# Three pairs of down tiles as seven products of quarters behind a plain part, in the two feed-forward blocks of a decoder step

## The chip, the cores and the metric

One NeuronCore of a Trainium2 chip runs the whole program. The metric is the device time of one execution in microseconds, the median of the runs shown. The profile is of one execution, taken by the hardware profiler; its times are counted from the start of its span. "Line" is a line of the kernel before, as the profile names it, if nothing else is said.

## What is computed

The program is one step of a hybrid decoder layer, in fp32, for 560 tokens at once: 512 of a prompt, 32 of running sequences and 16 meta tokens. Two feed-forward blocks (FFN1, FFN2) stand around a mixer of two attention branches. What matters here is this of the reference:

```
def swiglu(x, w_gate, w_up, w_down):
    return (jax.nn.silu(x @ w_gate) * (x @ w_up)) @ w_down

    h = x + 0.5 * rms_norm(swiglu(rms_norm(x, ffn1_pre_g), ffn1_w_gate, ffn1_w_up, ffn1_w_down), ffn1_post_g)
    ...
    y = h + 0.5 * rms_norm(swiglu(rms_norm(h, ffn2_pre_g), ffn2_w_gate, ffn2_w_up, ffn2_w_down), ffn2_post_g)
```

The model width is 1024 and the hidden width 2816. `@ w_down` is the down stage: 22 k-tiles of 128 hidden rows, and 8 tiles of 128 output columns.

## The kernel before

**Layout and precision.** Activations lie transposed, features on the 128 partitions and tokens along a row. A row of 560 tokens (544 in FFN2, which no longer needs the meta tokens) is cut in two halves, `h` = 0 and 1. Each fp32 factor is cut into a high part, rounded to fp32r by a cast on ScalarE, and the low rest, a subtraction on VectorE. A product of a weight tile and a moving tile is three matmuls: high by high, high by low, low by high.

**The down stage.** `k_steps` (lines 686 to 698) does one tile of output columns over a chunk of k-tiles. One k-tile is a **step**: six matmuls for both halves (lines 694 and 695 per half, then 697 per half), or three for one. `by_chunks` cuts each tile into chunks of 8, 7 and 7 k-tiles. The first two tiles go chunk by chunk side by side, since the hidden k-tiles 8 to 21 get their high and low parts only while those two run. Tiles 0 to 3 (0 to 4 in FFN2) are done for both halves; of the rest the first half is done for all tiles, then the second half for all, in the reverse order, so that the norm of the first half can start early. Its outputs come from `Norm`: `tile` squares and scales each finished tile on ScalarE (lines 738 and 739) and adds the squares up on VectorE; `start` sums them by matmuls with ones (lines 755 and 756) and takes the root; `add` scales and adds to `hT`, the residual h.

**What sets the order.** PE (TensorE), DVE (VectorE), ACT (ScalarE) and POOL run in the order in which the program is written; SP's transfers are ordered by a scheduler. `step()` is called after each k-tile and starts what `later(n, f)` had put off by n steps. The engines take their instructions in that order and wait by semaphores.

**Weights.** `Chunks` holds the list of weight tiles to come. `fetch` issues one transfer into one of three `raw` buffers (line 185, or two by line 620 for "quarters"). `split` casts the oldest raw to one of three `hi` buffers (ACT, line 660) and takes the `lo` part three steps later (DVE, line 152, the helper `tt`, which all two-operand operations share). In the down stage each chunk begins with one split and one fetch.

**Seven products.** The gate and up tiles and some gates of the mixer already use a product of two 2 x 2 block matrices in seven products instead of eight. The blocks of the moving matrix are a11, a21, a12, a22 (two halves of tokens by two halves of k), those of the weights two tiles by two halves of k. `weights_at` puts the four weight sums (DVE), the casts (ACT, line 855) and the lows at fixed steps; four sums s1 to s4 of moving blocks are made ahead; seven products of 4 k-tiles at 3 matmuls follow, in 14 steps, and their results are added up on DVE.

**h.** During the gate and up stage `hT`, 8 tiles of 128 x 560, is parked in DRAM (`h_dram`) and its room reused. `other_tiles` fetches it back in its last lines (line 1187), at the start of the down stage.

**Room.** `Arena` hands out pieces of SBUF ("room") by rules on which piece has been free longest. PSUM has two sets of four banks, "acc" and "ps".

Of the kernel before, what the change touches and what calls it, by code (L numbers as in the profile page):

```python
# [40 lines left out]
KEEP = 5  # L41
SUMS_BACK = (80, 86, 92, 102)
MIXER = [("R", "r", n) for n in range(3, 8)]
# [77 lines left out]
def hybrid_step(  # L121
# [158 lines left out]
    class Gates:  # L280


        def __init__(self, hd):
            self.hd = hd
# [415 lines left out]
    todo, vheld = [], []  # L700
    GATES, ROWS, EARLY = 6, 1, {3: 2}

    F0, F1 = (5, 13, 20), (5, 11, 14)
    LATE, MIX = (12, 22), (2, 4)

# [10 lines left out]
    def later(n, f):  # L716
        todo.append([n, f])
# [5 lines left out]
    class Norm:  # L723
# [37 lines left out]
        def add(self, h, g):  # L761
            w, n = self.wid[h], len(self.SETS[g])
            y, x = self.view(h, g), hT_room[g][:, : n * NT].rearrange("p (k t) -> p k t", t=NT)[:, :, h * HW : h * HW + w]
# [58 lines left out]
    def hidden(f, sl, at, nw, wid, hid, pairs):  # L822

        hi, lo = take(NT, F32R, True), take(NT, F32R, True)
        if pairs is None:
            for h, p in enumerate(zip(arena.halves(hi), arena.halves(lo))):
                hid.t[f, h] = p
        else:
            pairs[f] = hi, lo
            for h in range(2):  # L830
                c = slice(h * HW, h * HW + wid[h])
# [140 lines left out]
    def other_tiles(old, gain, rs, nw, wid, hid, pairs, plan, late, sums_at, begun):  # L972
# [210 lines left out]
        for i in range(len(waiting) + 3):  # L1183
            later(2 * i + 1, lambda: waiting and hidden(*waiting.pop(0), 1, nw, wid, hid, pairs))
        hT[:], hT_room = whole(KD)
        for k in range(KD):
            nc.sync.dma_start(hT[k], h_dram[k])

    CUTS = [(0, 8), (8, 15), (15, 22)]
    wd = ffn1_w_down[0]  # L1190

    order = [(n, (0, 1)) for n in range(4)] + [(n, (0,)) for n in range(4, 8)] + [(n, (1,)) for n in range(7, 3, -1)]
    DOWN = [(n, (0, 1)) for n in range(5)] + [(n, (0,)) for n in range(5, 8)] + [(n, (1,)) for n in range(7, 4, -1)]

    def by_chunks(order):

        both = [(n, hs, j) for j in range(3) for n, hs in order[:2]]
        return both + [(n, hs, j) for n, hs in order[2:] for j in range(3)]
# [4 lines left out]
    st.todo += [(wd, CUTS[j][0] * P, (CUTS[j][1] - CUTS[j][0]), P * n, P, False) for n, hs, j in by_chunks(order) if (n, hs) != (7, (1,))]  # L1203
    st.todo += [(win, r0, 4, c, 2 * P, 1 < n < 6) for n, (r0, c) in enumerate(vrows)]
# [12 lines left out]
    gate_up_weights(PLAN2, ffn2_w_gate[0], ffn2_w_up[0], 0)  # L1217
    st.todo += [(ffn2_w_down[0], CUTS[j][0] * P, (CUTS[j][1] - CUTS[j][0]), P * n, P, False) for n, hs, j in by_chunks(DOWN) if (n, hs) != (7, (1,))]
    E = mybir.EngineType
    with tc.manual_schedule(engines={E.PE, E.DVE, E.Activation, E.Pool}):  # L1220
# [164 lines left out]
        last, accs = {}, {}  # L1385
        for n, hs, j in by_chunks(order):
            if j == 0:
# [767 lines left out]
    with tc.manual_schedule(engines={E.PE, E.DVE, E.Activation, E.Pool}):  # L2155
# [222 lines left out]

        nd, last, accs = Norm(half2, W2), {}, {}
        ys = y_sample.rearrange("b t d -> (b t) d")  # L2380
# [11 lines left out]

        for n, hs, j in by_chunks(DOWN):
            if j == 0:
                accs[n, hs] = {h: ps("acc") for h in hs}
# [7 lines left out]
            k_steps(acc, parts, k0, k1, KF, hid, hs, wid=W2)  # L2403
            if j < 2:
                continue
            for h in hs:
                later(1, lambda n=n, h=h, acc=acc: nd.tile(n, h, acc[h]))
            if (n, hs) == (7, (0,)):
                later(2, exp_ln_table)
                later(F1[0], lambda: nd.start(0))  # L2410
                for g in range(3):
                    later(F1[1] + 12 * g, lambda g=g: nd.add(0, g))
                    for j in range(2):
                        later(F1[1] + 12 * g + 7 + 4 * j, lambda j=j, g=g: out(j, g))
        for p in pairs.values():
# [37 lines left out]
```

## Time and profile before

| | |
|---|---|
| median of 3 runs | 1515.96 us (1514.38 to 1517.47) |
| the profiled execution, its own time | 1509.63 us |
| its span, and mean granted TensorE clock | 1507.9 us, 0.999 |
| FFN1, down stage | 267.1 to 402.6 us of the span |
| FFN2, down stage | 1359.7 us to the tail, which begins at 1494.7 us |

The profile's page gives each engine's busy time and the chain of work that ended last, followed back from the end. Views of the trace give the rest: who waited for whom; stretches, with each engine's busy time, the granted clock and the DMA's share; groups of equal instructions, with their count, busy time and the mean duration of one in ns; and the instructions in order of time. There the first number of a row is its start, the second its duration (of all xN together), and what stands in brackets is the idle time of its engine just before, and what ended it. PE is TensorE, DVE VectorE, ACT ScalarE, SP the engine that issues most transfers.

### The profile page before, as it was taken

The numbers are of one execution on the slowest core, as the hardware profiler recorded it, in microseconds if no ns is written. First come the engines' busy times: TensorE is split into PE (matmuls) and PEld (weight loads), VectorE is DVE, ScalarE is ACT, GpSimd is POOL, SyncE is SP. The second block draws the span as 40 slices with busy tenths as digits, with TensorE's granted clock in tenths as the row PEclk, the third lists the DMA queues.
The fourth block names the chain that finished last, engine by engine and source line by source line (L and its number), as shares of the span: only waits on it lengthen the run. The fifth ranks groups of instructions, "written<-read, shape, count | busy, mean of one in ns | idle before, by whom it ended". The sixth has DMA issues, their size and how long they took to land.

```text
span 1507.9 us, 29580 instructions
## 1 busy us (share of the span) xinstructions
PE 1495.4 (99%) x11959; PEld 1444.0 (96%) x11959; DVE 1038.6 (69%) x1831; ACT 758.5 (50%) x1400; POOL 149.1 (10%) x216
## 2 busy tenths in 40 slices
PE   9999999999999999999999999999999999999998
PEld 8999999999999889899988999999999999999997
DVE  5888888523787857777776534977567888885234
ACT  6445454433665657565555443534564554544234
POOL 2000000000000111123224651000000000000000
PEclk9999999999999999999999999999999999999999
DMA  8123334524655473334455668434531343334343
GB/s 250 55 86 99 98 98 137 145 77 131 161 138 154 124 108 84 92 83 119 126 105 131 189 195 194 110 96 136 168 111 50 101 145 110 99 97 118 90 116 99
DMA packets 279561, 181.84 MB, mean 121 GB/s; under 512 B 10154, under 2 KB 264416, under 8 KB 279424
## 3 DMA queue, kind: packets, MB, share of 16 engines
q1 hardware_dynamic: 273968, 163.09, 41.0%
q0 software_dynamic: 5440, 16.85, 3.1%
q8 instruction: 94, 1.54, 0.4%
q14 instruction: 43, 0.35, 0.1%
q10 hardware_dynamic: 16, 0.00, 0.0%
HBM read 157.17 MB, written 22.74 MB: 119 GB/s over the span
## 4 chain that ended last, share of the span: by engine, by line
PE 95%; DVE 2%; DMA 1%; ACT 1%; issue 0%; SPq 0%; DVEq 0%; ACTq 0%
PE acc L694 10%; PE acc L697 10%; PE acc L695 10%; PE acc L681 8%; PE acc L1146 8%; PE acc L1144 8%; PE acc L1145 8%; PE acc L682 7%; PE acc L684 7%; PE acc L1087 2%; PE acc L1084 2%; PE acc L1085 2%; PE ps L1779 1%; PE acc L924 1%; PE acc L925 1%; PE acc L926 1%
## 5 line engine op out<-in xcount | busy, mean ns | idle before, releaser
L152 DVE TENSOR_TENSOR lo<-raw,hi 128x1024 fp32r<-128x1024 f32 (+1 forms) x216 | 258.6, 1198 | 174.8 <-ACT hi L660 166.3
L152 DVE TENSOR_TENSOR room<-room,room 128x544 fp32r<-128x544 f32 (+16 forms) x367 | 237.4, 669 | 122.4 <-ACT room L738 55.7
L681 PE MATMUL acc<-room,hi 128*128 128x280 f32 (+1 forms) x928 | 271.4, 309 | 0.1
L1146 PE MATMUL acc<-room,lo 128*128 128x280 f32 (+1 forms) x896 | 259.5, 290 | 0.0
L1145 PE MATMUL acc<-room,hi 128*128 128x280 f32 (+1 forms) x896 | 259.3, 289 | 0.0
L1144 PE MATMUL acc<-room,hi 128*128 128x280 f32 (+1 forms) x896 | 259.1, 289 | 0.0
L682 PE MATMUL acc<-room,hi 128*128 128x280 f32 (+1 forms) x928 | 250.5, 289 | 0.0
L694 PE MATMUL acc<-room,hi 128*128 128x280 f32 (+1 forms) x784 | 222.0, 292 | 0.0
L695 PE MATMUL acc<-room,hi 128*128 128x280 f32 (+1 forms) x784 | 219.0, 290 | 0.0
L660 ACT CAST hi<-raw 128x1024 fp32r<-128x1024 f32 (+1 forms) x130 | 131.9, 1015 | 145.0 <-PE acc L695 125.3
L684 PE MATMUL acc<-room,lo 128*128 128x280 f32 (+1 forms) x928 | 192.8, 289 | 0.0
L697 PE MATMUL acc<-room,lo 128*128 128x280 f32 (+1 forms) x784 | 192.3, 290 | 0.0
L681 PEld LDWEIGHTS acc<-room,hi 128*128 128x128 f32 x928 | 174.9, 188 | 13.0 <-issue 11.0
L682 PEld LDWEIGHTS acc<-room,hi 128*128 128x128 f32 x928 | 175.1, 189 | 2.8 <-issue 1.9
L1146 PEld LDWEIGHTS acc<-room,lo 128*128 128x128 f32 x896 | 168.6, 188 | 0.0
L1144 PEld LDWEIGHTS acc<-room,hi 128*128 128x128 f32 x896 | 168.6, 188 | 0.0
L1145 PEld LDWEIGHTS acc<-room,hi 128*128 128x128 f32 x896 | 168.4, 188 | 0.0
L694 PEld LDWEIGHTS acc<-room,hi 128*128 128x128 f32 x784 | 147.6, 188 | 2.0 <-issue 0.9
L695 PEld LDWEIGHTS acc<-room,hi 128*128 128x128 f32 x784 | 147.6, 188 | 0.2
L684 PEld LDWEIGHTS acc<-room,lo 128*128 128x128 f32 x928 | 145.0, 188 | 0.0
L855 ACT CAST hi<-raw 128x1024 fp32r<-128x1024 f32 x86 | 90.1, 1052 | 107.8 <-PE acc L1145 47.0
L697 PEld LDWEIGHTS acc<-room,lo 128*128 128x128 f32 x784 | 134.0, 188 | 0.0
(352 smaller groups left out, 2858.2 us busy)
## 6 DMA issues: line engine op xcount, KB each, us to landing
raw<-in_w_in_dram SPq DMA_DIRECT2D x49, 512.0 KB, 7.2
raw<-in_ffn_w_down_dram SPq DMA_DIRECT2D x42, 448.0 KB, 3.9
raw<-in_ffn_w_gate_dram SPq DMA_DIRECT2D x64, 256.0 KB, 3.3
raw<-in_ffn_w_up_dram SPq DMA_DIRECT2D x64, 256.0 KB, 3.3
raw<-in_ffn_w_down_dram SPq DMA_DIRECT2D x21, 512.0 KB, 4.0
out_dram<-room SPq DMA_DIRECT2D x32, 256.0 KB, 3.1
raw<-in_w_in_dram SPq DMA_DIRECT2D x28, 256.0 KB, 4.3
h_dram<-room SPq DMA_DIRECT2D x24, 280.0 KB, 3.1
```

The lines of the kernel that those rows point to most:

```text
L152: (eng or V).tensor_tensor(out=out, in0=a, in1=b, op=op)
L660: S.copy(h_, src)
L681: T.matmul(acc[h][:, : wid[h]], hi[k], a[h][0], start=(k == 0), stop=False)
L682: T.matmul(acc[h][:, : wid[h]], hi[k], a[h][1], start=False, stop=False)
L684: T.matmul(acc[h][:, : wid[h]], lo[k], a[h][0], start=False, stop=(k == KD - 1))
L694: T.matmul(acc[h][:nw, : wid[h]], wh, a[h][0], start=(k == 0), stop=False)
L695: T.matmul(acc[h][:nw, : wid[h]], wh, a[h][1], start=False, stop=False)
L697: T.matmul(acc[h][:nw, : wid[h]], wl, a[h][0], start=False, stop=(k == kt - 1))
L855: S.copy(hi[:, :kt], src)
L1144: T.matmul(x[:, :QW], hi, act[k][0], start=(first and k == 0), stop=False, skip_group_check=True)
L1145: T.matmul(x[:, :QW], hi, act[k][1], start=False, stop=False, skip_group_check=True)
L1146: T.matmul(x[:, :QW], lo, act[k][0], start=False, stop=(k == 3), skip_group_check=True)
```

## The change

Tiles 2 and 3 of FFN1, and tiles 2 and 3 and tiles 4 and 5 of FFN2, are each done as a pair. k-tiles 8 to 21 are done plainly into four PSUM banks (28 steps), k-tiles 0 to 7 as seven products of quarters (14 steps): four go to banks of their own, three are accumulated onto the plain parts. The results are combined on VectorE and go to `Norm.tile` from SBUF. The moving sums are made once per stage (`Down.pieces`), from step 14 on in groups of 8 steps, while tiles 0 and 1 run: per group two sums of a high and a low part (560 or 544 wide), four of quarters (280 or 272 wide), two casts, two lows. FFN2's halves become 272 and 272 tokens instead of 280 and 264.

h is fetched back (`h_again`) two steps after FFN1's pair and two steps after FFN2's last pair. An early fetch of a value chunk of the mixer moves from tile 3 to tile 4 of FFN1 (`EARLY`). The first half's outputs at the end are 9 steps apart instead of 12, since only four half tiles are left there. Saved sums of the mixer come back at its steps 80, 88, 96 and 104 instead of 80, 86, 92 and 102.

```diff
-SUMS_BACK = (80, 86, 92, 102)
+SUMS_BACK = (80, 88, 96, 104)
...
+    def h_again():
+        nonlocal hT_room
         hT[:], hT_room = whole(KD)
         for k in range(KD):
             nc.sync.dma_start(hT[k], h_dram[k])
 
+    class Down:
+        CUTS = ((8, 15), (15, 22))
...
+        def weights(cls, w, n):
+            a, b = (w[:, P * i : P * i + P] for i in (n, n + 1))
+            plain = [(w, k0 * P, k1 - k0, P * i, P, False) for k0, k1 in cls.CUTS for i in (n, n + 1)]
+            return plain + [((a, b), 0, KD, 0, P, "quarters"), ((b, a), 4 * P, KD, 0, P, "quarters")]
...
+        def pieces(self, start, every):
+            for i in range(4):
+                n = start + every * i
+                for d, f in ((0, lambda i=i: self.joined(i, 0)), (1, lambda i=i: self.joined(i, 1)), (2, lambda i=i: self.summed(i)),
+                             (4, lambda i=i: self.sums_hi(i, 0)), (5, lambda i=i: self.sums_hi(i, 1)),
+                             (6, lambda i=i: self.sums_lo(i, 0)), (7, lambda i=i: self.sums_lo(i, 1))):
+                    later(n + d, f)
+
+        def pair(self, n, tags, last):
...
+            weights_at(when, 28, key)
+            for d in (-5, -1):
+                later(42 + d, st.split)
+                later(42 + d + 1, st.fetch)
...
+            for m, g in ((3, lambda: copied("e1", a)), (5, lambda: copied("e5", d)), (7, lambda: add("u2", "e1", b)),
+                         (9, lambda: [add("x", "u2", c), add("u2", "u2", o["e5"]), add("e5", "x", o["e5"]),
+                                      add("e5", "e5", acc[n + 1, 1])]),
+                         (10, lambda: end("e5", n + 1, 1)), (11, lambda: add("e1", "e1", acc[n, 0])),
+                         (12, lambda: end("e1", n, 0)), (13, lambda: add("u2", "u2", acc[n + 1, 0])),
+                         (14, lambda: end("u2", n + 1, 0)), (15, lambda: add("x", "x", acc[n, 1])), (16, lambda: end("x", n, 1))):
+                later(m, g)
...
+            for x, act, part, k0, first in ((a, a11, "b1", 0, True), (d, s1, "b1", 4, True), (b, s2, "t", 0, True),
+                                            (c, s3, "t", 4, True), (acc[n, 0], a12, "b2", 4, False),
+                                            (acc[n + 1, 0], s4, "b2", 0, False), (acc[n, 1], a22, "t4", 0, False)):
+                for k in range(4):
...
-    order = [(n, (0, 1)) for n in range(4)] + [(n, (0,)) for n in range(4, 8)] + [(n, (1,)) for n in range(7, 3, -1)]
-    DOWN = [(n, (0, 1)) for n in range(5)] + [(n, (0,)) for n in range(5, 8)] + [(n, (1,)) for n in range(7, 4, -1)]
+    order1 = [(0, (0, 1)), (1, (0, 1)), "S2"] + [(n, (0,)) for n in range(4, 8)] + [(n, (1,)) for n in range(7, 3, -1)]
+    order2 = [(0, (0, 1)), (1, (0, 1)), "S2", "S4"] + [(n, (0,)) for n in range(6, 8)] + [(n, (1,)) for n in range(7, 5, -1)]
...
-        nd, last, accs = Norm(half2, W2), {}, {}
+        nd, last, accs = Norm(half2, (NW // 2, NW // 2)), {}, {}
...
-                    later(F1[1] + 12 * g, lambda g=g: nd.add(0, g))
+                    later(F1[1] + 9 * g, lambda g=g: nd.add(0, g))
```

How this moves instructions is seen at three places of FFN1. The rows are in the order of one engine: line, operation, what is written and read, size. First VectorE while tiles 0 and 1 run, between the lows of two weight chunks, before:

```order
L152 TENSOR_TENSOR lo239_3201<-raw230_3084,hi239_3200 128x896
L152 TENSOR_TENSOR room8_9_138<-room20_21_317,room1_32_912 128x560
L152 TENSOR_TENSOR room21_22_318<-room4_5_70,room8_9_138 128x560
L152 TENSOR_TENSOR room21_22_318<-room18_30_848,room21_22_318 128x560
L152 TENSOR_TENSOR room23_24_374<-room20_21_317,room23_24_374 128x560
L152 TENSOR_TENSOR lo241_3263<-raw232_3116,hi241_3262 128x896
```

And the same stretch after:

```order
L152 TENSOR_TENSOR lo239_3191<-raw230_3084,hi239_3190 128x896
L152 TENSOR_TENSOR room8_9_138<-room20_21_317,room1_32_912 128x560
L152 TENSOR_TENSOR room22_34_3215<-room4_5_70,room8_9_138 128x560
L152 TENSOR_TENSOR room17_18_252<-room24_27_431 128x560
L152 TENSOR_TENSOR room5_6_71<-room1_32_912,room8_9_138 128x560
L152 TENSOR_TENSOR room22_34_3215<-room18_30_848,room22_34_3215 128x560
L152 TENSOR_TENSOR room20_21_317<-room17_18_252,room5_6_71 128x280
L152 TENSOR_TENSOR room2_3_68<-room17_18_252 128x280
L152 TENSOR_TENSOR room20_21_317<-room20_21_317,room17_18_252 128x280
L152 TENSOR_TENSOR room2_3_68<-room5_6_71,room20_21_317 128x280
L152 TENSOR_TENSOR room15_28_612<-room20_21_317,room15_28_612 128x560
L152 TENSOR_TENSOR lo241_3260<-raw232_3116,hi241_3259 128x896
```

Before, the four rows in between are lows of hidden k-tiles. After, two rows of 560 and four of 280, the first group of moving sums, have come among them, and the lows behind them stand that much later in the queue.

Second, VectorE where tile 3 ends and the first half tile begins; `lo261` (before) and `lo267` (after) are the lows of that half tile's first chunk. Before:

```order
L152 TENSOR_TENSOR lo259_3634<-raw252_3477,hi259_3633 128x896
L152 TENSOR_TENSOR lo261_3694<-raw254_3537,hi261_3693 128x1024
L152 TENSOR_TENSOR lo263_3742<-raw256_3585,hi263_3741 128x896
L152 TENSOR_TENSOR room4_5_70<-room4_5_70,room6_7_72 128x280
L152 TENSOR_TENSOR room5_6_71<-room5_6_71,room17_18_252 128x280
L152 TENSOR_TENSOR lo266_3791<-raw260_3636,hi266_3790 128x896
```

After, from the result of the fourth product on (`ps` are the plain parts' banks):

```order
L152 TENSOR_TENSOR room17_18_252<-room17_18_252,acc264_3717 128x280
L152 TENSOR_TENSOR room17_18_252<-room17_18_252 128x280 x2
L152 TENSOR_TENSOR room17_18_252<-room17_18_252,ps252_3508 128x280
L152 TENSOR_TENSOR room6_7_72<-room6_7_72,room4_5_70 128x280
L152 TENSOR_TENSOR room17_18_252<-room17_18_252,ps249_3505 128x280
L152 TENSOR_TENSOR lo267_3783<-raw256_3568,hi267_3782 128x1024
L152 TENSOR_TENSOR room5_6_71<-room5_6_71,room4_5_70 128x280
L152 TENSOR_TENSOR room17_18_252<-room17_18_252,ps251_3507 128x280
L152 TENSOR_TENSOR room5_6_71<-room5_6_71,room2_3_68 128x280
L152 TENSOR_TENSOR room17_18_252<-room17_18_252,ps250_3506 128x280
L152 TENSOR_TENSOR lo269_3824<-raw258_3675,hi269_3823 128x896
```

The lows of the half tile's first two chunks now stand behind the additions that end the pair. The fourth, seventh and ninth row add squares, and so wait for ScalarE.

Third, SP where h comes back. Before, around the end of the gate and up stage:

```order
L185 DMA raw220_2960<-in_ffn1_w_down_dram 128x8x128
L1187 DMA room22_33_983<-h_dram_105 128x560 x2
L185 DMA raw227_3014<-in_ffn1_w_down_dram 128x7x128
L1187 DMA room14_35_3119<-h_dram_105 128x560 x2
L343 DMA room14_35_3119<-in_state_gla_dram 128x2x256
L1358 DMA room4_5_70<-in_w_in_dram 128x8x16
L185 DMA raw230_3084<-in_ffn1_w_down_dram 128x7x128
L1187 DMA room15_34_3118<-h_dram_105 128x560 x3
L185 DMA raw232_3116<-in_ffn1_w_down_dram 128x7x128
```

After, where the pair has ended (line 1191 is `h_again` in the changed kernel, 633 the value chunk; `raw268`, `raw270` and `raw273` are the three chunks of the second half tile):

```order
L185 DMA raw265_3725<-in_ffn1_w_down_dram 128x7x128
L1191 DMA room23_39_3857<-h_dram_105 128x560
L633 DMA room21_38_3839<-in_w_in_dram 128x4x256
L1191 DMA room23_39_3857<-h_dram_105 128x560
L185 DMA raw268_3795<-in_ffn1_w_down_dram 128x8x128
L1191 DMA room23_39_3857<-h_dram_105 128x560
L185 DMA raw270_3833<-in_ffn1_w_down_dram 128x7x128
L185 DMA raw273_3844<-in_ffn1_w_down_dram 128x7x128
L1191 DMA room3_40_3858<-h_dram_105 128x560 x3
L1191 DMA room20_41_3859<-h_dram_105 128x560 x2
L185 DMA raw275_3890<-in_ffn1_w_down_dram 128x8x128
```

The eight transfers of h no longer stand between the fetches of tiles 0 and 1, but between those of the half tiles.

More of the change, by code (lines that the diff above doesn't have):

```diff
@@ L822, in hidden @@
     def hidden(f, sl, at, nw, wid, hid, pairs):
-        hi, lo = take(NT, F32R, True), take(NT, F32R, True)
+        hi, lo = hid.full[f] = take(NT, F32R, True), take(NT, F32R, True)
         if pairs is None:
@@ L1195, in by_chunks, with down_weights @@
     def by_chunks(order):
-        both = [(n, hs, j) for j in range(3) for n, hs in order[:2]]
-        return both + [(n, hs, j) for n, hs in order[2:] for j in range(3)]
+        r = [(n, hs, j) for j in range(3) for n, hs in order[:2]]
+        for t in order[2:]:
+            r += [(int(t[1]), None, 0)] if t[0] == "S" else [(*t, j) for j in range(3)]
+        return r
+    def down_weights(w, order):
+        for n, hs, j in by_chunks(order):
+            if hs is None:
+                st.todo += Down.weights(w, n)
+            elif (n, hs) != (7, (1,)):
+                st.todo.append((w, CUTS[j][0] * P, CUTS[j][1] - CUTS[j][0], P * n, P, False))
@@ L1385, in hybrid_step @@
         last, accs = {}, {}
-        for n, hs, j in by_chunks(order):
+        down1 = Down(hid, NT, n1)
+        down1.pieces(*DSUMS1)
+        for n, hs, j in by_chunks(order1):
+            if hs is None:
+                down1.pair(n, ("ps", "acc"), True)
+                later(2, h_again)
+                continue
             if j == 0:
```

102 lines of the change are left out of this document (93 added, 9 removed).

## The prediction

> **What bounds the kernel now.** The page comes first: busy shares, then the chain that ended last.
>
> ```profile
> PE 1495.4 (99%) x11959; PEld 1444.0 (96%) x11959; DVE 1038.6 (69%) x1831; ACT 758.5 (50%) x1400; POOL 149.1 (10%) x216
> PE 95%; DVE 2%; DMA 1%; ACT 1%; issue 0%; SPq 0%; DVEq 0%; ACTq 0%
> ```
>
> TensorE is busy nearly the whole span and carries 95% of the chain. So time can go only by giving it less work, and can come only by making it wait. Next, whom TensorE waited for, all its waits of over half a microsecond bar one at the start:
>
> ```profile
> PE ps L2388 <- DVE room L152: 3.2, 1, 3.2
> PE ps L1763 <- ACT room L1766: 2.3, 1, 2.3
> PE ps L2388 <- ACT room L2389: 0.7, 1, 0.7
> PE ps L1788 <- ACT room L1766: 0.7, 1, 0.7
> ```
>
> L2388 is the tail, L1763 and L1788 the mixer; no wait lies in a down stage. Then the two down stages as stretches (busy columns in the order PE, PEld, DVE, ACT, POOL; then the granted clock, DMA share, GB/s), with the first two tiles of FFN1 by themselves:
>
> ```profile
> 267.10:402.60 135.50, 135.50 (x1049) 135.22 (x1048) 62.97 (x80) 58.97 (x94) 0.66 (x3) 1.00 0.45 126
> 267.10:301.00 33.90, 33.90 (x266) 33.90 (x265) 18.01 (x24) 15.30 (x25) 0.00 (x0) 1.00 0.52 152
> 1359.70:1495.00 135.30, 135.30 (x1080) 135.02 (x1078) 52.51 (x63) 50.10 (x83) 0.00 (x0) 1.00 0.37 107
> ```
>
> TensorE fills both at full clock; VectorE and ScalarE are under half busy. That is the room the change wants to use.
>
> **What goes.** A pair of tiles took 2 x 22 x 6 = 264 matmuls. It now takes 2 x 14 x 6 = 168 plain ones and 7 x 4 x 3 = 84 in the products: 12 fewer, 36 in all three; the order of TensorE's instructions bears the count out, and is otherwise unchanged outside the two stages. Twelve matmuls are two steps; TensorE's rows at the start of a step and two steps later, FFN1 first, then FFN2:
>
> ```profile
> 267.08 0.29 PE L694 MATMUL acc<-room,hi 128*128 128x280 f32 x1
> ...
> 268.62 0.29 PE L694 MATMUL acc<-room,hi 128*128 128x280 f32 x1
> ```
> ```profile
> 1361.23 0.29 PE L694 MATMUL acc<-room,hi 128*128 128x280 f32 x1
> ...
> 1362.74 0.29 PE L694 MATMUL acc<-room,hi 128*128 128x280 f32 x1
> ```
>
> So 1.54 us for the pair of FFN1, 1.51 us for each of FFN2: **4.56 us** leave the path. (A step is 0.77 us there, 0.755 here, half that for one half.) FFN2's widths of 280 and 264 become 272 twice, the same sum.
>
> [...]
>
> **Moving sums under the first pair: VectorE's queue.** VectorE runs in order, and the sums stand among the lows of k-tiles 8 to 21, for which the first two tiles wait. The prices, and the queue as it ran, FFN1 then FFN2 (in brackets idle time and its releaser):
>
> ```profile
> L152 DVE TENSOR_TENSOR room<-room,room 128x560 fp32r<-128x560 f32 x14 | 9.6, 738 | 0.0
> L152 DVE TENSOR_TENSOR room<-room,room 128x280 f32<-128x280 f32 x12 | 5.4, 451 | 21.7 <-ACT room L738 21.7
> ```
> ```profile
> 270.81 0.29 DVE L152 TENSOR_TENSOR room<-room,gains 128x128 f32<-128x128 f32 x1 [4.62 <-DMA room<-in_w_in_dram]
> ...
> 285.83 1.09 DVE L152 TENSOR_TENSOR lo<-raw,hi 128x896 fp32r<-128x896 f32 x1 [1.73 <-ACT hi L660]
> 286.85 1.38 DVE L152 TENSOR_TENSOR room<-room,room 128x560 fp32r<-128x560 f32 x2
> ```
> ```profile
> 1366.71 1.09 DVE L152 TENSOR_TENSOR lo<-raw,hi 128x896 fp32r<-128x896 f32 x1 [1.03 <-ACT hi L660]
> ...
> 1372.69 1.09 DVE L152 TENSOR_TENSOR lo<-raw,hi 128x896 fp32r<-128x896 f32 x1 [2.35 <-ACT hi L660]
> ...
> 1377.94 1.09 DVE L152 TENSOR_TENSOR lo<-raw,hi 128x896 fp32r<-128x896 f32 x1 [1.62 <-ACT hi L660]
> 1378.95 1.35 DVE L152 TENSOR_TENSOR room<-room,room 128x544 fp32r<-128x544 f32 x2
> ```
>
> Ahead of the last low (k-tile 21) now stand two of the four groups of sums, 8 x 0.738 + 8 x 0.451 = 9.5 us. In FFN2 that low ended at 1380.30; 5.0 us of the queue's idle time takes up part, so it comes at 1384.8. TensorE needs it in step 36, at 1359.7 + 36 x 0.755 = 1386.9: free by 2 us. In FFN1 it ended at 288.23; plus 9.5 less 1.73 is 296.0, against a need at 267.08 + 36 x 0.77 = 294.8. That would be 1.2 us late, unless the first row's 4.62 us of waiting shrink: that load stood amid the h transfers, which are gone from there. I expect them to shrink by 2 us and take **0**, between 0 and 1.2. The whole group, 19 us per stage, then has to end before step 76, with the pair's 28 plain steps to spare. ScalarE's casts of the sums are 8 x 0.66 us in a stage where it is under half busy.
>
> **After a pair: the hand-off.** Let T be the end of the fourth product. Three more products run, 6 steps, 4.62 us; then a half tile with steps of 0.385. Its first chunk's low stands in VectorE's queue behind six adds, one of which waits for ScalarE's square. Prices: square, post-scaling, adds, casts and lows.
>
> ```profile
> 296.52 0.40 ACT L738 ACTIVATE room<-acc 128x280 f32<-128x280 f32 x1
> 296.81 0.49 ACT L739 ACTIVATE room<-acc,half_post 128x280 f32<-128x280 f32 x1
> ```
> ```profile
> L152 DVE TENSOR_TENSOR room<-room,acc 128x280 f32<-128x280 f32 x64 | 28.4, 444 | 10.8 <-PE acc L1146 8.6
> ```
> ```profile
> L152 DVE TENSOR_TENSOR lo<-raw,hi 128x896 fp32r<-128x896 f32 x22 | 23.9, 1089 | 18.1 <-ACT hi L660 18.1
> L152 DVE TENSOR_TENSOR lo<-raw,hi 128x1024 fp32r<-128x1024 f32 x11 | 13.5, 1224 | 28.2 <-ACT hi L660 28.2
> ```
> ```profile
> L660 ACT CAST hi<-raw 128x896 fp32r<-128x896 f32 x22 | 20.6, 941 | 44.4 <-PE acc L695 43.9 <-PE acc L1145 0.5
> L660 ACT CAST hi<-raw 128x1024 fp32r<-128x1024 f32 x11 | 11.5, 1048 | 17.4 <-PE acc L695 16.8 <-ACT room L739 0.5
> ```
>
> Four adds 1.8, square 0.4, two adds 0.9, low 1.22, and 0.2 for the first's start: T + 4.5. TensorE loads that low at T + 4.62 + 0.13 = 4.75. The second chunk's follows after four more adds, a square and its own 1.09: T + 7.8, needed at T + 4.62 + 8 x 0.385 + 0.13 = 7.83. No cover is left, but nothing is late: I take **0**, up to 1.5 where post-scaling (0.49) and cast (0.94) also get in between. It decides twice, in FFN1 and at FFN2's last pair; FFN2's first pair is followed by whole steps. The weight sums (four of 128x512, twelve in all) have 10 steps before their first product.
>
> **h fetched later.** Taken away from the start of the down stage it gains nothing: no wait of TensorE's lies there. Where it now stands, half tiles eat a chunk in 3 us, and SP's order puts two h transfers and the value chunk before the next chunk's fetch (three h in FFN2). What such transfers did when they ran together at the end of the gate and up stage, and alone:
>
> ```profile
> 258.00:260.00 2.00, 2.00 (x18) 2.00 (x17) 1.28 (x2) 0.93 (x3) 0.00 (x0) 1.00 0.90 278
> 260.00:262.00 2.00, 2.00 (x18) 2.00 (x17) 1.14 (x2) 0.37 (x2) 0.00 (x0) 1.00 0.92 251
> ```
> ```profile
> raw<-in_ffn_w_down_dram SPq DMA_DIRECT2D x21, 512.0 KB, 4.0
> ```
>
> The fetch for the tile after the half tile can start when the first low is done, T + 4.5. Ahead are 2 x 0.287 (128 x 560 x 4 bytes) + 0.524 = 1.1 MB issued from T + 2, 4.1 us at 265 GB/s; behind them its own 0.524 MB, 2.0 us, or 4.0 us alone from T + 4.5: landed by T + 8.5. The next tile starts at T + 4.62 + 22 x 0.385 = 13.1; cast and low take 2.3, so T + 10.8 does. **0**, with 2 us to spare. The h itself is needed over 20 us later. Value chunk, returned mixer sums and room numbers change no order on TensorE outside the down stages: 0.
>
> **The tail.** The last half is 272 wide instead of 264, 3%:
>
> ```profile
> 1494.72 0.61 PE L755 MATMUL ps<-room,ones 128*128 128x264 f32 x2
> ...
> 1495.36 0.71 PE L756 MATMUL ps<-room,ones 128*128 128x264 f32 x2
> 1496.11 0.48 ACT L758 ACTIVATE room<-ps,epst 128x264 f32<-128x264 f32 x1 [0.43 <-PE ps L756]
> 1496.62 0.42 ACT L759 ACTIVATE room<-room 128x264 f32<-128x264 f32 x1
> 1497.08 5.28 DVE L152 TENSOR_TENSOR room<-room,room 128x792 f32<-128x792 f32 x6 [7.80 <-ACT room L759]
> ```
>
> 3% of these 7.5 us is 0.2; some is fixed or hidden: **+0.15** (0.05 to 0.2). The first half's outputs, now 9 steps apart, end 4 steps before the last matmul, as they must.
>
> **Sum.** -4.56 + 0.15 = -4.4 us. The profiled execution took 1509.63 us (span 1507.9 and 1.7 around it), so 1505.2; against the median of the runs, 1515.96, **1511.6**. A measurement tells about 0.2%, 3.0 us, from no change.
>
> **Rivals.**
> - *The hand-off is late.* Twice 1.5 us: -4.4 + 3.0, 1514.5. For it: no cover by the durations. Against: successive instructions of one engine start before the one ahead ends (296.52 + 0.40, next at 296.81). 0.20.
> - *VectorE's queue under FFN1's first pair.* 1.2 us: 1512.8. 0.07.
> - *Slower: weights behind the whole h burst.* If all eight h and the value chunk, 2.8 MB, pass before the next chunk, it lands at T + 2 + 10.6 + 2.0 = 14.6, 3.8 us late; FFN2 with 2.3 MB 2.1 late: 5.9. A TensorE that idles loses clock, as the row below shows for the tail: 4 us at about 0.8 after each is 1.6 more. -4.4 + 7.5: 1519.1. It decides once 10.8 - 8.5 = 2.3 us of delay are passed. SP's order speaks against it. 0.09.
> - *The mixer's two waits (2.3 + 0.7) fall away*, as rooms move: 1508.6. 0.05.
>
> ```profile
> 1498.00:1502.00 4.00, 2.04 (x13) 1.79 (x14) 3.90 (x6) 1.21 (x3) 0.00 (x0) 0.84 0.22 80
> ```
>
> [...]
>
> **How the numbers follow.** My forecast has the remaining 0.59, with 1510.0 to 1513.2 from the runs' own spread of 1.5 us. The range must leave out no more than 0.2: from 1508.6, the last rival, to 1515.8, the late hand-off and the runs' spread; the slower rival stays out. Faster: nine tenths of the forecast, the mixer case, half of the second rival, a little of the first: 0.62. Slower: 0.10. Same: 0.28.
>
> **What would show it.** Right: no wait for L152 or a cast before a down matmul; PE busy 4 to 5 us less; VectorE busier by some 60 us at no cost (38 of moving sums; an estimate of 24 for weight sums, lows and adds at the prices above). Hand-off wrong: TensorE idle before the first half tile's low weights. h wrong: ScalarE's cast waiting for a DMA there. Wrong altogether: a wait on h rooms, or seven products whose matmuls are not 125 to 128 ns apart.

## The result, and the profile after

| | us |
|---|---|
| before, median of 5 runs beside the changed kernel | 1515.96 (1514.38 to 1517.47) |
| changed, median of 5 runs | 1510.00 (1509.95 to 1510.18) |
| ratio, 95% interval | 0.9962 (0.9950 to 0.9974) |
| changed, profiled execution | 1510.10, span 1508.4 |

6.0 us faster, about 0.4%; forecast 1511.6 (1508.6 to 1515.8). The result lies in the range, but the two profiles say at once that not all of its reasons can be right: the profiled execution of before took 1509.63, so between the *profiles* nothing was gained. The page of the changed kernel, busy row and chain:

```profile
PE 1494.6 (99%) x11923; PEld 1440.9 (96%) x11923; DVE 1090.8 (72%) x1934; ACT 773.3 (51%) x1425; POOL 149.0 (10%) x216
PE 95%; DVE 2%; DMA 1%; ACT 1%; issue 0%; ACTq 0%; DVEq 0%; SPq 0%
```

36 matmuls fewer, VectorE 52 us busier (forecast about 60), the same chain. Of the 4.6 us that TensorE should lose only 0.8 is gone. The waits of TensorE, without the start's, two of 0.3 us and two of 0.2:

```profile
PE ps L2531 <- DVE room L152: 4.0, 2, 3.2
PE ps L2115 <- issue: 2.1, 5, 0.4
PE acc L697 <- DVE lo L152: 1.3, 2, 0.7
...
PE acc L694 <- ACT hi L660: 0.3, 1, 0.3
```

L2531 is the tail, as before. The two waits of the mixer, on a ScalarE room, are gone; new are L2115 in the mixer ("issue": nothing that it waited for shows in the profile) and two lines in a down stage. The down stages as stretches:

```profile
267.27:403.70 136.43, 134.84 (x1037) 133.88 (x1036) 87.01 (x126) 66.57 (x106) 0.66 (x3) 1.00 0.49 136
1362.80:1494.80 132.00, 132.00 (x1053) 131.84 (x1052) 80.17 (x120) 57.04 (x95) 0.00 (x0) 1.00 0.38 111
```

FFN2 went about as forecast, 135.3 to 132.0, full (the two stretches do not end at quite the same instruction; by the marks below it is 2.88 us). FFN1 was 135.50 and is 136.43 with 1.6 us of holes. The rest has to be found stage by stage. Outside the down stages TensorE's order is the same, so the first and last L694 matmul of each run of them mark stages; their rows in the changed kernel:

```profile
267.27 0.29 PE L694 MATMUL acc<-room,hi 128*128 128x280 f32 x1
...
460.56 0.29 PE L694 MATMUL acc<-room,hi 128*128 128x280 f32 x1
...
1071.49 0.29 PE L694 MATMUL acc<-room,room 128*128 128x280 f32 x1
...
1362.82 0.28 PE L694 MATMUL acc<-room,hi 128*128 128x272 f32 x1
...
1494.57 0.28 PE L694 MATMUL acc<-room,hi 128*128 128x272 f32 x1
```

and in a second profile of the kernel before (the first experiment; 1516.37 us, span 1514.7):

```profile
267.83 0.29 PE L694 MATMUL acc<-room,hi 128*128 128x280 f32 x1
...
460.05 0.29 PE L694 MATMUL acc<-room,hi 128*128 128x280 f32 x1
...
1075.40 0.29 PE L694 MATMUL acc<-room,room 128*128 128x280 f32 x1
...
1366.42 0.29 PE L694 MATMUL acc<-room,hi 128*128 128x280 f32 x1
...
1501.05 0.28 PE L694 MATMUL acc<-room,hi 128*128 128x264 f32 x1
```

Differences of neighbouring rows, with the same points of the first profile of before (267.08, 459.31, 1068.71, 1359.73, 1494.36):

| stage, us | before, 1st profile | before, 2nd profile | changed |
|---|---|---|---|
| to FFN1's down stage | 267.08 | 267.83 | 267.27 |
| FFN1 down and the first products behind it | 192.23 | 192.22 | 193.29 |
| mixer | 609.40 | **615.35** | 610.93 |
| FFN2 gate and up | 291.02 | 291.02 | 291.33 |
| FFN2 down | 134.63 | 134.63 | 131.75 |
| to the end of the span | 13.5 | 13.7 | 13.8 |

Read this way: the kernel before is the same everywhere to 0.8 us except in its mixer, where one execution took 6 us more than the other. The one that the forecast was made from was the short one; the runs lie at the long one. Against the long one the change gives 1.07 us away in FFN1, takes 2.9 in FFN2, and 4.4 in the mixer, which the forecast had at zero.

### The profile page after: what moved, and what is told of

It reads as the page before. It is cut to its first block, busy times and chain, and to the rows that moved or that the text cites. A ratio compares the mean times of both kernels' runs of the same rounds, so it can differ in the third digit from the quotient of the medians.

```text
span 1508.4 us, 29660 instructions
## 1 busy us (share of the span) xinstructions
PE 1494.6 (99%) x11923; PEld 1440.9 (96%) x11923; DVE 1090.8 (72%) x1934; ACT 773.3 (51%) x1425; POOL 149.0 (10%) x216
## 3 DMA queue, kind: packets, MB, share of 16 engines
q8 instruction: 94, 1.54, 0.4%
## 4 chain that ended last, share of the span: by engine, by line
PE 95%; DVE 2%; DMA 1%; ACT 1%; issue 0%; ACTq 0%; DVEq 0%; SPq 0%
PE acc L681 8%; PE acc L1147 8%; PE acc L1145 8%; PE acc L682 8%; PE acc L684 8%; PE acc L1146 8%; PE acc L694 7%; PE acc L697 7%; PE acc L695 7%; PE acc L1088 2%; PE acc L1085 2%; PE acc L1086 2%; PE acc L925 1%; PE acc L927 1%; PE acc L926 1%; PE ps L1920 1%
## 5 line engine op out<-in xcount | busy, mean ns | idle before, releaser
L152 DVE TENSOR_TENSOR room<-room,room 128x544 fp32r<-128x544 f32 (+17 forms) x419 | 266.2, 658 | 89.1 <-ACT room L760 27.9
L681 PE MATMUL acc<-room,hi 128*128 128x280 f32 (+1 forms) x928 | 271.2, 309 | 0.2 <-DVE room L155 0.2
L1147 PE MATMUL acc<-room,lo 128*128 128x280 f32 (+1 forms) x896 | 259.8, 290 | 0.0
L1146 PE MATMUL acc<-room,hi 128*128 128x280 f32 (+1 forms) x896 | 259.2, 289 | 0.0
L1145 PE MATMUL acc<-room,hi 128*128 128x280 f32 (+1 forms) x896 | 259.1, 289 | 0.0
L682 PE MATMUL acc<-room,hi 128*128 128x280 f32 (+1 forms) x928 | 250.4, 289 | 0.0
L684 PE MATMUL acc<-room,lo 128*128 128x280 f32 (+1 forms) x928 | 192.7, 289 | 0.0
L681 PEld LDWEIGHTS acc<-room,hi 128*128 128x128 f32 x928 | 174.8, 188 | 13.1 <-issue 11.0
L682 PEld LDWEIGHTS acc<-room,hi 128*128 128x128 f32 x928 | 175.1, 189 | 2.8 <-issue 1.9
L1147 PEld LDWEIGHTS acc<-room,lo 128*128 128x128 f32 x896 | 168.6, 188 | 0.0
L1145 PEld LDWEIGHTS acc<-room,hi 128*128 128x128 f32 x896 | 168.5, 188 | 0.0
L1146 PEld LDWEIGHTS acc<-room,hi 128*128 128x128 f32 x896 | 168.5, 188 | 0.0
L684 PEld LDWEIGHTS acc<-room,lo 128*128 128x128 f32 x928 | 145.0, 188 | 0.0
L694 PE MATMUL acc<-room,hi 128*128 128x280 f32 (+2 forms) x498 | 143.0, 294 | 0.3 <-ACT hi L660 0.3
L695 PE MATMUL acc<-room,hi 128*128 128x280 f32 (+2 forms) x498 | 140.9, 290 | 0.0
L697 PE MATMUL acc<-room,lo 128*128 128x280 f32 (+2 forms) x498 | 127.8, 291 | 1.3 <-DVE lo L152 1.3
L856 ACT CAST hi<-room 128x1024 fp32r<-128x1024 f32 x84 | 70.2, 836 | 81.0 <-PE acc L1146 59.1
L694 PE MATMUL acc<-room,room 128*128 128x280 f32 (+3 forms) x366 | 107.8, 295 | 0.0
L152 DVE TENSOR_TENSOR lo<-room,hi 128x1024 fp32r<-128x1024 f32 x84 | 80.2, 955 | 37.0 <-ACT hi L856 36.8
```

The lines of the kernel that those rows point to most:

```text
L152: (eng or V).tensor_tensor(out=out, in0=a, in1=b, op=op)
L681: T.matmul(acc[h][:, : wid[h]], hi[k], a[h][0], start=(k == 0), stop=False)
L682: T.matmul(acc[h][:, : wid[h]], hi[k], a[h][1], start=False, stop=False)
L684: T.matmul(acc[h][:, : wid[h]], lo[k], a[h][0], start=False, stop=(k == KD - 1))
L694: T.matmul(acc[h][:nw, : wid[h]], wh, a[h][0], start=(k == 0), stop=False)
L695: T.matmul(acc[h][:nw, : wid[h]], wh, a[h][1], start=False, stop=False)
```

## The experiments

Each run was timed in turn with the kernel before on the same chip; runs of one group share it. Before was at 1515.69 (21 runs) beside the first four, at 1511.81 (22) beside the next four, at 1511.17 (9) beside the last. So differences to before are compared, not times across groups.

### Where does before scatter, and is it the mixer's order?

**Before once more.** No edit.

> The kernel before, unchanged, to get a second profile of it. Its unprofiled runs lay at 1514.4 to 1517.5 us, its one profiled execution at 1509.6. Theory (the page gathers of the mixer, 804 to 900 us, decide the difference from execution to execution): median again 1515 to 1517, scatter 2 us or more; if the second profiled execution is 1512 us or longer, what it has more than the first lies between 800 and 930 us, as waits of TensorE in front of L1763, L1788 or L1974, and not in the feed-forward stages, which agree to 0.3 us. Rival (profiling itself shortens it): profiled again 1509.6 within 0.5 while the runs stay near 1516. Rival (elsewhere): the added time lies in a feed-forward stage, the start or the tail.

Measured: 1516.28 us (1513.21 to 1517.51, 11 runs), ratio 1.0005 (0.9996 to 1.0014); profiled 1516.37. The table shows that all but 0.85 us of the 6.8 between the two profiles lies in the mixer. Its waits there:

```profile
PE ps L1763 <- ACT room L1766: 2.6, 1, 2.6
PE ps L1974 <- issue: 2.3, 4, 1.0
...
PE ps L1788 <- ACT room L1766: 0.7, 1, 0.7
```

L1763 waits 0.3 us longer than in the first profile, and L1974 (products with the gathered values, 2.3) is new. A third loss (1.7) is no wait at all; what is left of the stage's 5.95 us stands in no row shown here. In stretches of this profile the granted clock, third column from the end, falls behind L1763's wait:

```profile
818.00:820.00 2.00, 0.29 (x3) 0.31 (x3) 0.00 (x0) 0.91 (x2) 0.94 (x3) 1.00 0.78 280
820.00:822.00 2.00, 1.28 (x8) 1.05 (x6) 1.46 (x2) 1.44 (x3) 0.00 (x0) 0.64 0.11 43
822.00:824.00 2.00, 2.00 (x11) 2.00 (x11) 2.00 (x5) 0.04 (x1) 0.00 (x0) 0.50 0.21 53
824.00:826.00 2.00, 2.00 (x13) 1.14 (x14) 1.90 (x7) 0.65 (x2) 0.00 (x0) 1.00 0.43 126
```

In the first profile it held:

```profile
818.00:820.00 2.00, 0.64 (x5) 0.43 (x5) 0.53 (x1) 1.98 (x4) 0.20 (x1) 1.00 0.45 174
820.00:822.00 2.00, 2.00 (x17) 2.00 (x18) 2.00 (x4) 0.75 (x3) 0.00 (x0) 1.00 0.09 27
```

The trace's record of the clock has it at half from 820.57 to 823.98, 3.41 us at 0.50, so an estimated 1.7 us of work late. The first profile's record begins at 5.67 us, with full clock to 1500.71, half to 1504.12, full to 1507.53 and half again: 1495.04, 3.41 and 3.41 us, which are 438, 1 and 1 times 3.413. The changed kernel's has the same 1495.04 us of full clock, from 6.14 on. So I divide each execution into windows of 3.413 us, counted from the start of a stretch in its own record; that they bear on the clock is my reading, as no run was made to try it. In the window just before the fall TensorE was busy for 0.52 us here. In the first profile, counted from its 5.67, the wait fell into two windows, with 1.72 and 2.10 us of work, and the clock stayed at 1.00:

```profile
817.16:820.57 3.41, 0.52 (x3) 0.31 (x3) 0.03 (x1) 1.48 (x3) 1.78 (x4) 1.00 0.73 254
```
```profile
814.63:818.04 3.41, 1.72 (x15) 1.50 (x13) 0.00 (x0) 0.02 (x1) 2.98 (x5) 1.00 0.92 338
818.04:821.46 3.42, 2.10 (x16) 1.90 (x17) 1.99 (x3) 2.33 (x4) 0.19 (x1) 1.00 0.28 108
```

What is behind the wait of L1763 is in the chain of the second profile:

```profile
810.04 8.88 DMA out_dram<-room
...
819.09 0.09 ACT room L1766
```

ScalarE's copy L1766 writes into a room whose last content is still on its way to an output in memory, 8.9 us from its issue, amid the page gathers (804.82 to 816.90 us by GpSimd's rows in the first profile). TensorE waits for the copy.

**Only the steps at which the mixer's sums are fetched back.**

```diff
-SUMS_BACK = (80, 86, 92, 102)
+SUMS_BACK = (80, 88, 96, 104)
```

> The kernel before with one line of the change alone: the steps of the mixer at which its returned sums are fetched (80, 88, 96, 104 instead of 80, 86, 92, 102); no pair, h fetched where it was. Theory (part of the 6 us is the mixer's order of fetches, not the pairs): 1511 to 1514 us, scatter under 1 us. Rival (all of it is the pairs): 1515 to 1517, as before. Rival (the line costs, being needed only for room): above 1517.

Measured: 1516.13 us (1515.43 to 1516.88, 11 runs), ratio 1.0003 (0.9994 to 1.0012). The line alone does nothing; my theory of it fell. Its profile has L1763 at 3.0, L1974 at 2.3 and the half clock as well.

**Both kernels without the page gathers.** GpSimd sets the rooms to zero, so the sample rows are not the reference's.

```diff
         t = ring.pop(0)
-        G.indirect_dma_start(out=t, out_offset=None, in_=src,
-                             in_offset=bass.IndirectOffsetOnAxis(ap=idx[c][:, i : i + 1].bitcast(U32), axis=0))
+        G.memset(t, 0.0)
```

> The kernel before without the gathers of the cached keys and values in the mixer (GpSimd sets their rooms to zero instead; the sample rows of the output are then not the reference's). Theory (the gathers make the scatter): 1505 to 1508 us, all runs within 0.7 us, profiled execution and runs agree within 1 us; the waits of 2.3 and 0.7 us at L1763 and L1788 may go too. Rival (scatter comes from elsewhere): runs still scatter by 2 us or more and lie 4 us or more above the profiled execution.

> The changed kernel without the gathers, in the same way. Theory: the three gaps of 0.6 to 0.7 us at 841 to 843 us and the two at 876 and 893 (L2115) go, so 1506 to 1507.5 us; against the kernel before without gathers it is 1.2 to 2.2 us faster, which is what the feed-forward stages of the two traces give (FFN1 0.9 us slower, FFN2 2.8 us faster). Rival (the pairs do give 4.4 us, and the profile of before was an odd one): 3.9 us or more faster than the kernel before without gathers.

Measured: before without gathers 1506.71 us (1505.94 to 1506.87), ratio 0.9943 (0.9930 to 0.9957); changed without gathers 1505.59 (1505.04 to 1506.49), ratio 0.9936 (0.9923 to 0.9950). The runs lie within 0.9 and 1.5 us, and none of the mixer's waits is left. The change is then worth 1.1 us, just under what the stages gave (1.2 to 2.2 expected), not 4.4. So five of the six us hang on the gathers.

### The parts of the change

By the two programs, the copy at L1766 for the last head pair waits for two DMA queues before, and for none in the changed kernel (in the latter's trace it waits for TensorE alone): rooms are given out by when they were last freed, FFN1's new code frees others, and this copy gets a different room.

**Before, with that room alone chosen otherwise.**

```diff
+            other = [take(512) for _ in range(1 if (self.pr, e, n) == (7, 0, 1) else 0)]
             t = take(512)
+            give(*other)
             (V.tensor_copy if e else S.copy)(t[:, :c], p[:, :c])
```

> The kernel before with one room chosen otherwise: for the last head pair of the mixer, ScalarE's copy at L1766 that waited 2.3 to 3.0 us for an output transfer out of its room takes the next free room instead. No pair, no later fetch of h. Theory (most of the 6 us is this wait, the half clock that follows it where it is long, and what queues behind it among the gathers): 1510.5 to 1513 us, no granted clock below 1.0 between 800 and 930 us. Rival (the gathers set the pace there, and the waits come back at L1974): 1515 to 1517.

Measured: 1506.97 us (1506.34 to 1507.43, 6 runs) against 1511.81, ratio 0.9969 (0.9957 to 0.9981): **4.8 us**, without one product of the change. (The times expected in this group were reckoned from 1515.7 for before; as a difference, 2.7 to 5.2 was expected here.) TensorE between 800 and 930 us, in the second profile of before and here:

```profile
800.00:930.00 130.00, 124.30 (x1278) 114.79 (x1277) 60.40 (x142) 50.36 (x100) 58.35 (x63) 0.99 0.61 163
```
```profile
800.00:930.00 130.00, 129.84 (x1379) 121.66 (x1381) 62.03 (x138) 53.01 (x105) 58.12 (x61) 1.00 0.70 182
```

The wait, the half clock and L1974's waits are all gone. What the room saves here is a wait of 2.3 and one of 0.7 (below, the profile of FFN2's pairs, which keeps it) and 1.7 for the clock, 4.7. L1974's waits occur in no profile of this group or the next, not even in that one, so none of the 4.8 is theirs. By the marks of the stage table the mixer takes 606.0 us here and 611.3 in that profile, 5.3 more. The edit may move rooms given out later as well; every other stage agrees with before's first profile to 0.6 us.

**FFN2's pairs alone** (FFN1's order, h and value chunk as before):

```diff
-    order1 = [(0, (0, 1)), (1, (0, 1)), "S2"] + [(n, (0,)) for n in range(4, 8)] + [(n, (1,)) for n in range(7, 3, -1)]
+    order1 = [(n, (0, 1)) for n in range(4)] + [(n, (0,)) for n in range(4, 8)] + [(n, (1,)) for n in range(7, 3, -1)]
...
         list(feed1)
+        h_again()
```

> The changed kernel with FFN1's down stage as before (no pair, h at the start), FFN2's two pairs kept. By the program the copy in the mixer still waits for the output transfer. Theory: only FFN2's gain, 2.8 us by the two traces: 1512 to 1513.5 us, scatter as of the kernel before (2 us or more). Rival (the pairs as such give the 6 us): 4 us gained, 1511.7.

Measured: 1509.49 us (1508.42 to 1511.61, 11 runs), ratio 0.9986 (0.9977 to 0.9995): 2.3 us faster, and with the scatter of before. Its profile keeps the room's wait and loses the clock:

```profile
PE ps L1899 <- ACT room L1902: 2.3, 1, 2.3
```
```profile
820.00:822.00 2.00, 2.00 (x12) 2.00 (x12) 2.00 (x5) 0.36 (x2) 0.00 (x0) 0.60 0.16 26
```

The same 2.3 us cost the clock here and not in the first profile of before; the window of 3.41 us before the fall had 1.51 us of work:

```profile
816.98:820.39 3.41, 1.51 (x11) 1.31 (x12) 1.39 (x2) 2.35 (x4) 0.74 (x3) 1.00 0.45 154
```

**FFN1's pair alone** (FFN2's `order2` of whole tiles, `h_again()` behind `list(feed2)`, the widths of 272 kept):

> The changed kernel with FFN2's down stage as before (five whole tiles, h at the start, but widths of 272 twice), FFN1's pair kept. By the program the copy in the mixer no longer waits for a transfer. Theory: FFN1 0.9 us slower, the mixer 4 to 5 us faster than in the ordinary runs of before: 1512 to 1513.5 us, scatter under 1 us. Rival (FFN1's pair gives its 1.5 us and nothing else): 1514.2. Rival (FFN1's part costs): above 1516.

Measured: 1508.01 us (1507.46 to 1509.24, 11 runs), ratio 0.9975 (0.9966 to 0.9984): 3.8 us faster (2.2 to 3.7 expected as a difference, with a scatter under 1 us; it was 1.8). The room alone gives 4.8, so FFN1's pair with the moved h costs 1.0, as the table's 1.07 says. FFN1's part and FFN2's add to 6.1; the whole change gave 5.99 in the last group and 5.96 at first: the parts add up.

### What stops TensorE in FFN1?

The changed kernel: SP's issues behind the pair, ScalarE's cast of the second half tile's first chunk, and TensorE at that tile:

```profile
331.20 0.34 SPq L1191 DMA_DIRECT2D room<-h_dram  x1
331.59 0.43 SPq L633 DMA_DIRECT2D room<-in_w_in_dram  x1
332.06 0.50 SPq L1191 DMA_DIRECT2D room<-h_dram  x1
333.88 0.37 SPq L185 DMA_DIRECT2D raw<-in_ffn_w_down_dram  x1
```
```profile
341.66 1.05 ACT L660 CAST hi<-raw 128x1024 fp32r<-128x1024 f32 x1 [4.64 <-DMA raw<-in_ffn_w_down_dram]
```
```profile
342.76 0.40 PE L694 MATMUL acc<-room,hi 128*128 128x280 f32 x1 [0.26 <-ACT hi L660]
342.99 0.29 PE L695 MATMUL acc<-room,hi 128*128 128x280 f32 x1
344.02 0.40 PE L697 MATMUL acc<-room,lo 128*128 128x280 f32 x1 [0.74 <-DVE lo L152]
```

VectorE is the releaser in the last row, but it stands at the end of a chain: cast and low waited for the weights, issued at 333.88 and landed by 341.66. With matmuls 0.128 apart in a full stretch, starts 0.56, 0.24, 1.03 and 0.23 apart (342.20 to 344.25) are 1.5 us lost, and 0.85 more went the same way at 353.4. What the queue carried meanwhile:

```profile
332.00:334.00 2.00, 2.00 (x18) 2.00 (x17) 2.00 (x4) 1.49 (x4) 0.00 (x0) 1.00 0.77 210
334.00:336.00 2.00, 2.00 (x18) 2.00 (x17) 1.49 (x5) 1.90 (x4) 0.00 (x0) 1.00 0.53 109
336.00:338.00 2.00, 2.00 (x18) 2.00 (x17) 2.00 (x3) 1.02 (x3) 0.00 (x0) 1.00 0.41 122
338.00:340.00 2.00, 2.00 (x17) 2.00 (x17) 0.21 (x1) 0.00 (x0) 0.00 (x0) 1.00 1.05 342
```

Not too much traffic but too little: 109 to 122 GB/s for four us with transfers outstanding. By the size of its pieces it is the value chunk (512 pieces of 1024 bytes, 333.3 to 338.7); the weights' pieces of 512 bytes begin at 337.7.

**The value chunk at tile 6 instead of 4.**

```diff
-    GATES, ROWS, EARLY = 6, 1, {4: 2}
+    GATES, ROWS, EARLY = 6, 1, {6: 2}
```

> The changed kernel with the value chunk (half a MB of the mixer's weights) fetched two half tiles later, at tile 6 of FFN1; h as in the change. Theory (the chunk of 1024-byte pieces takes 5 us in the DMA queue, and the weights of the second half tile lie behind it): the stop of 1.5 us at 342.8 to 344.3 goes, that of 0.85 us at 353.4 may stay: 1507.5 to 1509 us. Rival (the h transfers do it): 1509.7 to 1510.3, stop unchanged. Rival (VectorE's queue at the hand-off, as the prediction had it): unchanged as well, with the stop's cause an add of VectorE.

Measured: 1503.10 us (1502.82 to 1504.83), ratio 0.9943 (0.9929 to 0.9956). The stops at 343 and 353 are gone, and the next weights behind the chunk stop TensorE in the same pattern:

```profile
360.02 0.40 PE L694 MATMUL acc<-room,hi 128*128 128x280 f32 x1 [0.49 <-ACT hi L660]
360.26 0.29 PE L695 MATMUL acc<-room,hi 128*128 128x280 f32 x1
361.28 0.40 PE L697 MATMUL acc<-room,lo 128*128 128x280 f32 x1 [0.73 <-DVE lo L152]
```

In this profile the stop follows the chunk; the h transfers have stayed. It is 8.7 us ahead of before (6.7 to 8.2 expected). But the profiled execution, 1504.83, is the slowest of the five and 1.7 us above their median, about what the stop costs (FFN1's stage 192.65 by the marks, against 190.89 below without a stop). So the other four may well have run without it, which only a second profile could show. The last group tells chunk and h apart, beginning with the changed kernel itself:

> The changed kernel, unchanged, beside the three others on one chip. The gain over the kernel before was 6.0 us on the first chip; on the chip where the parts ran, the room alone gave 4.8, FFN1's pair 3.8 with the room in it, FFN2's pairs 2.3. Theory (the parts add up): 5.5 to 6.5 us faster than the kernel before here, and FFN1's stops again 1.5 us at 342.8 to 344.3 and 0.85 us at 353.4. Rival (they don't add up, since the gathers take back what comes before them): 4 us or less.

```diff
-                later(2, h_again)
+                later(2, h_room)
+                for k in range(KD):
+                    later(24 + 6 * k, lambda k=k: nc.sync.dma_start(hT[k], h_dram[k]))
```

> The changed kernel with FFN1's eight h transfers issued one by one from step 24 on instead of together from step 2; value chunk as in the change. Theory (the value chunk's slow transfer holds back the weights of the second half tile, the h burst those of the third): the stop of 1.5 us at 343 stays at 0.8 to 1.6, that at 353 goes: 0.8 to 1.6 us faster than the changed kernel. Rival (the h transfers do both): both go, 2.4 us faster. Rival (the hand-off's VectorE queue): both stay.

```diff
-    GATES, ROWS, EARLY = 6, 1, {4: 2}
+    GATES, ROWS, EARLY = 6, 1, {7: 2}
```

> The changed kernel with the value chunk fetched at tile 7 of FFN1, behind which a half tile follows that needs no weights of its own; h together, as in the change. With the chunk at tile 6 the stops at 343 and 353 went and one of 1.8 us came at 360, at the first weights behind the chunk. Theory (the stop follows the chunk): no stop over 0.5 us in FFN1, 2 to 2.5 us faster than the changed kernel. Rival (the h burst too holds weights back by enough): a stop of 0.5 to 1 us near 343 or 353 stays, 1.2 to 1.9 us faster.

> Both edits: h one by one from step 24 on, value chunk at tile 7. Theory: as with the chunk alone at tile 7, within 0.4 us, since the chunk is the cause: 2 to 2.5 us faster than the changed kernel, no stop in FFN1. Rival (both are causes): 0.5 us or more faster than with the chunk alone.

| us (5 runs each) | value chunk at tile 4 | value chunk at tile 7 |
|---|---|---|
| h together | 1505.18 (1504.68 to 1506.35) | 1503.20 (1502.66 to 1503.54) |
| h one by one | 1504.85 (1504.77 to 1505.84) | **1502.89** (1502.52 to 1503.18) |

Before is at 1511.17; the ratios are 0.9962 (0.9948 to 0.9975), 0.9947 (0.9933 to 0.9960), 0.9959 (0.9945 to 0.9972) and 0.9944 (0.9931 to 0.9958). Moving the chunk gives 2.0 us in either row, and with it there, no wait is left in FFN1's down stage; spreading h gives 0.3, within the runs' own scatter, where 0.8 to 1.6 was expected. On SP's queue the first three h stayed where they were, so that edit spread the five behind them: the stop at 353 went, the one at 343 stayed and its first wait grew from 0.34 us (the changed kernel's profile in this group) to 0.67, so FFN1's stage gained only 0.5 (193.35 to 192.83):

```profile
343.07 0.40 PE L694 MATMUL acc<-room,hi 128*128 128x280 f32 x1 [0.67 <-ACT hi L660]
343.31 0.29 PE L695 MATMUL acc<-room,hi 128*128 128x280 f32 x1
344.33 0.40 PE L697 MATMUL acc<-room,lo 128*128 128x280 f32 x1 [0.73 <-DVE lo L152]
```

FFN1's down stage with the chunk at tile 7, h together:

```profile
267.01:401.30 134.29, 134.29 (x1039) 134.01 (x1038) 86.97 (x126) 66.75 (x106) 0.66 (x3) 1.00 0.49 138
```

135.5 before, 134.3 now and full: the pair's gain is there once the weights come in time. Both edits together are 8.3 us ahead of before and 2.3 ahead of the change; by their differences to before the runs do not tell them from the chunk alone at tile 7 (8.0) or at tile 6 (8.7).

## Why the forecast came out, step by step

| step of the sum | forecast | measured |
|---|---|---|
| FFN1's pair, matmuls | -1.54 | -1.34 (190.89 between the marks with the chunk at tile 7, 192.23 before) |
| FFN2's pairs, matmuls | -3.02 | -2.88 by the table; -2.3 as a kernel of their own |
| VectorE's queue under the first pair | 0 (to 1.2) | 0: no wait there in the profile |
| hand-off behind a pair | 0 (to 1.5) | 0: the first half tile runs through, in both stages |
| h and the value chunk later | **0** | **+2.4** |
| the mixer: rooms, SUMS_BACK | **0** | **-4.8** as a kernel of its own, -4.4 by the table |
| tail | +0.15 | +0.2 to +0.3 |

The sum of the right column is about -6, and that was the result; the forecast of -4.4 came within 1.6 us by luck: two steps that it had at nothing failed in opposite directions.

**"Landed by T + 8.5."** The time at which the weights are issued was right: the first half tile began at 333.85, so T is 329.23, and the fetch went out at T + 4.65 (forecast 4.5). They landed at T + 12.4 instead, 1.6 us behind the T + 10.8 that was granted. The term that was mis-sized is the value chunk, 0.524 MB at 265 GB/s, 2.0 us, from a stretch in which other kinds of transfers ran. The trace of before has this very transfer at its old place, in the view of its line:

```profile
DMA to landing us min/median/max: 6.5/6.5/6.5
```

6.5 us from issue to landing against 4.0, the median of the down stages' weight chunks of the same size. In the changed kernel its pieces ran from 333.3 to 338.7, 5.4 us, 3.4 more than the 2.0 of the sum; the weights behind it came 3.9 later than forecast. The slower rival named the right place and mechanism, weights late behind other transfers, but blamed the wrong one: it counted bytes.

**"Room numbers change no order on TensorE: 0."** True of the order, not of the waits. The rival in which the mixer's two waits fall away had 0.05 and a price of 3.0, their length in one profile. It happened, and the price was 4.8, since in the three other profiles that have it the wait is 2.3 to 3.0 us long, with one of 0.4 to 0.7 behind it, and the clock is at 0.50 for 3.41 us after it.

**The base.** The sum was made against one profiled execution and carried over to the runs as a difference. That execution lay 4.75 us below the lowest of the three runs shown, and the text only noted it. It had the room's wait, which was priced, but not the half clock behind it, nor L1974's waits, which both later profiles of the first group have; so the largest gain looked smaller than it was.

What sets L1974's (after: L2115's) waits from one execution to the next stays open: without gathers there are none, and none in the profiles of the last two groups, which ran on another chip than the first group. What they cost can be told by the marks. The mixer takes 605.9 to 606.3 us in all nine profiles that have neither these waits nor the room's; 610.9 in the first profile of the changed kernel, which has these alone; 611.3 in that of FFN2's pairs, which has the room's wait and the half clock alone; and 615.35 in before's second, which has both. So either is worth 4.0 to 5.3 us, and since L1974's (L2115's) were there on both sides of the stage table, its 4.4 us are by and large the room's wait with its clock.

One reading of the prediction is off without harm: it calls VectorE under half busy, but its own row for FFN1's first two tiles has 18.01 of 33.90 us, just over half.

## What to carry to other kernels

When a profiled execution lies clearly below the plain runs, get a second one and compare them stage by stage before pricing a change: what differs between two executions of one kernel is a cost that a change can remove or bring back. An allocator that hands out buffers by history makes every edit ahead of it an edit behind it; compare which waits on transfers appear and vanish in the program, not the order alone. Price a transfer by the row of that transfer, not by bytes over the rate of others, and look for what stands behind it in the same queue.

## What the runs showed of the hardware

- While a half-MB chunk in 1024-byte pieces was under way in the changed kernel (333.3 to 338.7 us), the DMA queue carried 109 to 122 GB/s for four us; at its old place in the kernel before it took 6.5 us from issue to landing. The down stages' weight chunks of the same size, in 512-byte pieces, took 4.0 in the median there. Why this chunk was slower was not tried.
- After a wait of TensorE of 2.3 to 3.0 us its clock was at 0.50 for 3.41 us in three of the four profiles that have it (before's second, that with the other fetch steps, FFN2's pairs alone); in before's first it held. The window of 3.41 us just before the fall had 0.52 us of work in before's second profile and 1.51 in that of FFN2's pairs. In before's first the two windows with the wait had 1.72 and 2.10, and no window from 60 to 1480 us had less; in the changed kernel's the least was 2.42, and the clock held at 1.00 in both to the tail. There the windows before the two falls of before's first profile had 1.17 and 0.29. How much work keeps the clock up was not tried.
- The kernel before took 1515.7 us beside the first group, on one chip, and 1511.2 to 1511.8 beside the others, on another, whose profiles show no stops at the products with gathered values; the change gained 6.0 us at either level (1515.96 and 1511.17 for before).
